# One encoder layer on one core: a sixth Strassen group in the input projection, tanh for the gates, bias and mask summed behind FFN 1, and weights cast and loaded earlier

## The chip, the core and the metric

The kernel runs on one core of one Trainium2 chip. Time is device time in microseconds (us) of one launch; a kernel's time is the median over its runs. The core has a matrix engine (PE), a vector engine (DVE), a scalar engine that evaluates functions (ACT), a general engine (POOL) and a queue processor that issues most transfers (SP). Each engine works through its own list of instructions in order; between engines they wait on semaphores.

## The reference

One layer of an encoder for 1024 tokens of width 1024, all in float32:

```python
h = x + 0.5 * swiglu(rms_norm(h, ffn1_norm), w_gate1, w_up1, w_down1)    # FFN 1, inner width 2816
u = rms_norm(h, mix_norm)
qa, ka, va, qb, kb, vb, ga, gb = split(u @ w_in)                          # 512 x 3, 512, 128, 128, 1024, 1024
ya = neighbourhood_attention_2d(qa, ka, va, na_rpb)     # 8 heads of 64; a learned bias per head and a window mask
yb = windowed_gqa_sink(rope(qb), rope(kb), vb, sink)    # 8 query heads, 2 key heads; a sink logit in the denominator
merged = sigmoid(ga) * (ya @ w_branch_a) + sigmoid(gb) * (yb @ w_branch_b)
h = h + merged @ w_out
h = h + 0.5 * swiglu(rms_norm(h, ffn2_norm), w_gate2, w_up2, w_down2)    # FFN 2
y = rms_norm(h, final_norm)
```

Tokens form a grid of 16 rows by 64 columns. In branch A a query sees a neighbourhood of 8 by 16 tokens, in branch B a band of 128 tokens to each side.

## The kernel before, in words

**Products in three parts.** A float32 operand is cast into a high part, and what is left is its low part (`split`, L93 the cast on ACT, L94 the subtraction on DVE, or on POOL where one is named). Each product is the sum of high by high, high by low and low by high: three matmuls, L145, L147 and L149 in `mm3`. PE writes into eight PSUM banks, four tagged `d` and four tagged `g`.

**Strassen.** Large matrix products run as seven block products (P1 to P7) in place of eight. `products` does this for a weight that is streamed in: the FFNs' gate and up weights, and the *groups* of the input projection. A group holds 4 of the 34 channel blocks of 128 channels that `w_in` has; its products are 7 x 2 x 4 x 3 = 168 matmuls of 128x512. Its weights land in `raw` or `ahead` tiles, ACT casts them (L309) and DVE subtracts (L312) into `ws` tiles, of which there are eight. `Down` does the FFNs' down products (and `w_out`): 7 products x 11 elements for the FFN; an element is one pair of left and right blocks with 12 matmuls of 128x512. `Down.prep` makes an element ready: load of the left block (L547), additions of the right blocks (L561, L563 on DVE; L564, L566 on POOL), two splits (L94). It runs RING = 7 elements ahead of PE. Functions in `loads` of an element are called in `run` just before that.

**Stages in time.** FFN 1 (to about 432 us), FFN 1 down (to 645), the transition with norm and transposes, the groups of the input projection (to 845), attention (to 1118), the rest of the branches, `w_out`, and FFN 2 from about 1180. `behind(prods)` runs group 0's first products between the transition's tokens, and loads the weights of groups 1 and 2 into `ahead` tiles (L286) at tokens 3 and 4; these tiles are of the `ws` kind.

**Attention.** 64 *units*: 32 of branch B (two heads, 128 queries each), then 32 of branch A. A unit is `scores` (two products per head, then a fused DVE step L1298 that adds bias or mask and takes the maximum, ACT's exp at L1301, DVE's reciprocal L1304 and scaling L1305), `turn` (transposes on PE, L1314, and splits of what they give, L94) and `values` (products, L1328 and L1333, then a copy of ACT, L1267, and additions of DVE, L1268 and L1271). Between the units `filling` feeds PE with *fill steps* from `filler`: first the channel blocks of ga and gb that are in no group ("gates", 8 steps of 6 matmuls 128x512 each), then `branch_b` (yb @ w_branch_b, 8 column blocks of 4 steps of 6 matmuls), then the start of branch A. There are 112 + 32 + 6 = 150 steps; 106 of them run between the units, 44 behind the last one. For each pair of heads of branch A, `load_bias` fetches the bias (made during FFN 1, in `bias_d`) and DVE adds the mask (L1088). `split_y` casts a block of ya or yb; it subtracts on POOL for six of the eight blocks.

**Order.** The order of instructions on each engine is that of the code, but for a scheduler that may move them within what the tiles allow; `pin` keeps an instruction in its place.

Of the kernel before, what the change touches and what calls it, by code (L numbers as in the profile page):

```python
# [36 lines left out]
def trunk_kernel(ctx, tc, x, xt, n1, wg1, wu1, wd1, nm, win, rpb, sink, wa, wb, wo,  # L37
# [54 lines left out]
    def split(dst_hi, dst_lo, src, eng=None):  # L92
        nc.scalar.copy(dst_hi, src)  # L93
        (eng or nc.vector).tensor_tensor(dst_lo, src, f32v(dst_hi), op=ALU.subtract)  # L94
# [139 lines left out]
    def products(src, n, after, at_end, extra, ring, by_hand=False, last=PRODUCTS):  # L234
# [34 lines left out]
        def load_ahead(i):  # L269

            for m in range(2):
                ahead[i, m] = main.tile([P, 1024], F32, tag="ws", bufs=8, name=nm_("ahead"))
                fetch(ahead[i, m], i, m, 0)
# [14 lines left out]
        def pieces(q):  # L288

            i, p, m = seq[q]  # L290
            if i and (i, p, m) in early:
                a = ahead[i, m][:, 512 if p == "P2" else 0:][:, :512]
# [95 lines left out]
    def behind(prods):  # L388

        run, load_ahead = prods[2:4]  # L390

        def post(t):
            if t >= 3:
                drain(run, 10)
            if t in (3, 4):
                load_ahead(t - 2)

        return post
# [278 lines left out]

    def behind_ffn1(n):
        down.at_end(n)
        if n <= 60 and spread:  # L680
            nc.sync.dma_start(*spread.pop(0))
# [194 lines left out]
    groups = [[(12, 13), (14, 15)], [(16, 17), (0, 1)], [(4, 5), (8, 9)], [(2, 3), (6, 7)], [(10, 11), (18, 19)]]  # L876
# [62 lines left out]

    pin = tc.keep_in_program_order  # L940
# [65 lines left out]

    def keep_u():

        h, l = rhs(T4)
        for i in range(2):  # L1010
            r = raw4()
            nc.sync.dma_start(r.rearrange("p (t f) -> p t f", t=2), u_d[2 * i:2 * i + 2].rearrange("t p f -> p t f"))
            cols = slice(i * 256, i * 256 + 256)
            v = [a[:, :, cols].rearrange("p c (t x) -> p c t x", t=2) for a in (h, l)]
            split(v[0], v[1], r.rearrange("p (t c x) -> p c t x", t=2, c=4))
# [41 lines left out]
    hook(2, gate_first)  # L1057
    hook(1, keep_u)
    pg = products(lambda i, m, half: w_cols(win[0], groups[i][m][half] * P), NG, store_z, at_end, (2, 3), range(8, 16),
                  last=("P1", "P2", "P5", "P6", "P7", "P4", "P3"))  # L1060
    down.into(transition(down1, gain, to_strassen, behind(pg), 2), pg)
# [4 lines left out]
    mask_a = masks[:, :768].rearrange("p (s k) -> p s k", s=2)  # L1066
    mask_b = masks[:, 768:]
    nc.sync.dma_start(mask_a, c_mask_a.rearrange("s p k -> p s k"))
# [12 lines left out]
    def bias_slot(s):  # L1081
        return fa[:, 768 * s:768 * s + 768].rearrange("p (e k) -> p e k", e=2)

    def load_bias(s, h):
        braw = raw4()[:, :384]
        nc.sync.dma_start(braw, bias_d[h])
        for e in range(2):
            nc.vector.tensor_tensor(bias_slot(s)[:, e, :].rearrange("p (d r w) -> p d r w", d=3, r=ROWS),  # L1088
                                    braw.rearrange("p (r d w) -> p d r w", d=3, w=8),
                                    mask_a[:, e, :].rearrange("p (d r w) -> p d r w", d=3, r=ROWS), op=ALU.add)  # L1090
# [58 lines left out]
    def branch_w(w, dc, eng=None, r=None):  # L1149

        t = ws4()
        if r is None:
            r = fetch_branch(raw4()[:, :512], w, dc)
        split(t[:, :512], t[:, 512:], r, eng)
# [15 lines left out]
    def split_y(slots, r0, eng):  # L1170
# [6 lines left out]
        split(h, l, r, eng)  # L1177

    a_order = [dc for p in range(4) for dc in (p, p + 4)]
    a_mm, a_raw = [], {}  # L1180

    def branch_a(i):

        w = branch_w(wa[0], a_order[i], nc.gpsimd, a_raw.get(i))
        bs = [bank("gd"[i % 2]) for _ in range(2)]
        a_mm.append((bs, branch_mm(bs, w, Y_A)))
# [4 lines left out]
    def gate_b(dc):  # L1191
        rb = xs4()
        nc.sync.dma_start(rb, g_d[D + dc * P:D + (dc + 1) * P, :])
        nc.scalar.activation(rb, rb, AF.Sigmoid)
        return rb

    def branch_b():

        for c in range(2, 4):
            split_y(Y_B[c], c * P, nc.vector if c == 2 else nc.gpsimd)  # L1200
        for g in (4, 6):
            new_ar(g, F32)
        nxt = branch_w(wb[0], 0, nc.vector), gate_b(0)
        for dc in range(NC8):
            w, rb = nxt
            bs = [bank("dg"[dc % 2]) for _ in range(2)]
            yield from branch_mm(bs, w, Y_B)
            if dc + 1 < NC8:
                nxt = branch_w(wb[0], dc + 1, nc.vector), gate_b(dc + 1)
            for n in range(2):  # L1210
                sl = slice(n * 512, (n + 1) * 512)
                nc.vector.tensor_tensor(merged(dc)[:, sl], bs[n], rb[:, sl], op=ALU.mult)

    def filler():
        for dc, nxt in zip(gates, gates[1:] + [None]):
            if nxt is not None:
                yield from gate(dc, {4: lambda: mix.update(gate=load_w(win[0], GA + nxt * P))})
            else:
                yield from gate(dc, {0: lambda: [fetch_y(c * P) for c in range(2)],
                                     4: lambda: [split_y(Y_B[c], c * P, nc.gpsimd) for c in range(2)],  # L1220
                                     5: lambda: [fetch_y(c * P) for c in range(2, 4)]})
        yield from branch_b()
        for i in range(2):
            branch_a(i)
            for _ in range(3):
                drain(a_mm[i][1], 1)
                yield

    fill = filler()
    nfill = len(gates) * 8 + 38  # L1230
# [7 lines left out]
    def units_b():  # L1238
        for j in range(NTT):
            for c in range(4):  # L1240
                def write(o, j=j, c=c):

                    if c == 0:
                        ybox["b"] = xs4()[:, :512].rearrange("p (c t) -> p c t", c=4)
                    lo = mix["lo"][:HD, c % 2]
                    nc.scalar.copy(lo, o[HD:])
                    for s in range(2):
                        nc.vector.tensor_tensor(ybox["b"][s * HD:s * HD + HD, c, :], o[:HD, s, :], lo[:, s, :], op=ALU.add)
                    if c == 3:
                        nc.gpsimd.dma_start(y_d[:512, j * P:(j + 1) * P].rearrange("(c p) t -> p c t", p=P), ybox["b"])  # L1250
# [4 lines left out]
                           sink=[nsk[:, 2 * c + s:2 * c + s + 1] for s in range(2)], write=write)  # L1255

    def units_a():
        for hp in range(4):
            qs, kd, kl, va = heads_a[hp]
            for s in range(2):  # L1260
                load_bias(s, 2 * hp + s)
            for j in range(NTT):
                def write(o, j=j, hp=hp):
# [8 lines left out]
                    if j in (3, 7) and hp < 3:  # L1272
                        cols = slice((j - 3) * P, (j + 1) * P)
# [298 lines left out]
```

## Time and profile before

| | us |
|---|---|
| median of 3 runs | 1932.24 |
| fastest to slowest | 1932.03 to 1932.97 |
| the profiled execution | 1934.2 |
| its span in the profile | 1932.4 |
| PE busy in it | 1921.6 |
| DVE, ACT, POOL busy | 1435.8, 943.4, 294.9 |

The profiled execution is one run with the hardware profiler on, 2.0 us above the median. Busy times of PE overlap, since matmuls are pipelined: what one costs is read from the distance of their starts. The same holds, in part, for DVE and ACT. An arrow in a row stands for what an engine waited for.

### The profile page before, as it was taken

The numbers are of one execution on the slowest core, as the hardware profiler recorded it, in microseconds if no ns is written. First come the engines' busy times: TensorE is split into PE (matmuls) and PEld (weight loads), VectorE is DVE, ScalarE is ACT, GpSimd is POOL, SyncE is SP. The second block draws the span as 40 slices with busy tenths as digits, with TensorE's granted clock in tenths as the row PEclk, the third lists the DMA queues.
The fourth block names the chain that finished last, engine by engine and source line by source line (L and its number), as shares of the span: only waits on it lengthen the run. The fifth ranks groups of instructions, "written<-read, shape, count | busy, mean of one in ns | idle before, by whom it ended". The sixth has DMA issues, their size and how long they took to land.

```text
span 1932.4 us, 25477 instructions
## 1 busy us (share of the span) xinstructions
PE 1921.6 (99%) x8956; PEld 1603.9 (83%) x8956; DVE 1435.8 (74%) x2560; ACT 943.4 (49%) x1826; POOL 294.9 (15%) x432
## 2 busy tenths in 40 slices
PE   9999999999999999999999999999999999999998
PEld 7888888888888888888888888888888888888886
DVE  7987765668957778678888856889676566569864
ACT  6532333344446543477778872365333333344453
POOL 0011110013400112211122222010111001005210
PEclk9999999999999999999999999999999999999999
DMA  6244323286333467653358675543422322493341
GB/s 262 100 167 162 130 106 126 87 292 224 89 109 135 161 202 239 218 163 104 106 135 197 190 241 207 175 153 120 147 93 104 131 86 106 144 356 99 113 143 61
DMA packets 151745, 298.70 MB, mean 155 GB/s; under 512 B 14912, under 2 KB 64448, under 8 KB 151616
## 3 DMA queue, kind: packets, MB, share of 16 engines
q1 hardware_dynamic: 123072, 210.53, 33.3%
q0 software_dynamic: 27824, 85.48, 13.2%
q8 instruction: 71, 1.16, 0.3%
q10 hardware_dynamic: 720, 1.05, 0.1%
q14 instruction: 58, 0.48, 0.1%
HBM read 210.50 MB, written 88.27 MB: 155 GB/s over the span
## 4 chain that ended last, share of the span: by engine, by line
PE 97%; DVE 1%; ACT 1%; DMA 1%; issue 0%; POOLq 0%; POOL 0%; DVEq 0%
PE g L145 18%; PE g L147 18%; PE g L149 18%; PE d L145 12%; PE d L149 12%; PE d L147 12%; PE d L1314 2%; PE g L1328 1%; PE d L1293 1%; PE d L1294 1%; PE g L1333 1%; PE d L138 1%; DMA ahead<-in_w_in_dram 0%; DVE ar L94 0%; DMA n1c<-in_ffn_norm_dram 0%
## 5 line engine op out<-in xcount | busy, mean ns | idle before, releaser
L145 PE MATMUL g<-ar,ws 128*128 128x512 f32 x1128 | 422.8, 395 | 0.6 <-DVE fa L602 0.6
L147 PE MATMUL g<-ar,ws 128*128 128x512 f32 x1128 | 417.1, 390 | 0.0
L149 PE MATMUL g<-ar,ws 128*128 128x512 f32 x1128 | 416.6, 390 | 0.0
L145 PE MATMUL d<-ar,ws 128*128 128x512 f32 x736 | 282.7, 391 | 0.4 <-ACT ws L309 0.4
L147 PE MATMUL d<-ar,ws 128*128 128x512 f32 x736 | 282.2, 390 | 0.4 <-DVE ar L813 0.3
L149 PE MATMUL d<-ar,ws 128*128 128x512 f32 x736 | 281.9, 390 | 0.0
L147 PEld LDWEIGHTS g<-ar,ws 128*128 128x128 f32 x1128 | 211.8, 188 | 44.9 <-DVE ar L834 0.4
L149 PEld LDWEIGHTS g<-ar,ws 128*128 128x128 f32 x1128 | 211.8, 188 | 45.0
L145 PEld LDWEIGHTS g<-ar,ws 128*128 128x128 f32 x1128 | 206.4, 188 | 36.7 <-ACT ar L93 1.0
L312 DVE TENSOR_TENSOR ws<-raw,ws 128x512 fp32r<-128x512 f32 x204 | 139.5, 690 | 99.1 <-ACT ws L309 98.1
L309 ACT CAST ws<-raw 128x512 fp32r<-128x512 f32 x204 | 125.0, 620 | 142.1 <-PE g L149 64.0
L147 PEld LDWEIGHTS d<-ar,ws 128*128 128x128 f32 x736 | 138.4, 188 | 30.0 <-DVE ar L813 1.3
L145 PEld LDWEIGHTS d<-ar,ws 128*128 128x128 f32 x736 | 138.4, 188 | 29.4 <-ACT ws L309 0.8
L149 PEld LDWEIGHTS d<-ar,ws 128*128 128x128 f32 x736 | 138.5, 188 | 29.2 <-DVE ws L312 0.5
L93 ACT CAST ws<-raw 128x512 fp32r<-128x512 f32 (+1 forms) x121 | 81.0, 669 | 144.1 <-PE d L149 63.7
L94 DVE TENSOR_TENSOR ws<-raw,ws 128x512 fp32r<-128x512 f32 (+1 forms) x119 | 93.2, 785 | 60.0 <-ACT ws L93 59.6
L415 POOL DMA_DIRECT2D hid<-fx x91 | 49.1, 540 | 432.0 <-DVE fx L475 287.9
L93 ACT CAST ar<-raw 128x512 fp32r<-128x512 f32 (+1 forms) x83 | 56.1, 679 | 94.3 <-PE g L147 55.0
L94 DVE TENSOR_TENSOR ws<-ar,ws 128x512 fp32r<-128x512 f32 x114 | 98.2, 867 | 2.8 <-ACT ws L93 2.8
L145 PE MATMUL g<-ws,ws 128*128 128x512 f32 x232 | 90.9, 392 | 0.0
L149 PE MATMUL g<-ws,ws 128*128 128x512 f32 x232 | 90.5, 390 | 0.0
L147 PE MATMUL g<-ws,ws 128*128 128x512 f32 x232 | 90.4, 390 | 0.0
(313 smaller groups left out, 3606.9 us busy)
## 6 DMA issues: line engine op xcount, KB each, us to landing
raw<-hid SPq DMA_DIRECT2D x70, 512.0 KB
hid<-fx POOLq DMA_DIRECT2D x91, 256.0 KB, 2.3
ar<-in_ffn_w_down_dram SPq DMA_DIRECT2D x32, 512.0 KB
raw<-in_ffn_w_up_dram SPq DMA_DIRECT2D x31, 512.0 KB
raw<-in_ffn_w_gate_dram SPq DMA_DIRECT2D x27, 512.0 KB
raw<-in_w_in_dram SPq DMA_DIRECT2D x27, 512.0 KB
hid<-fa POOLq DMA_DIRECT2D x51, 256.0 KB, 2.6
ar<-zs_d POOLq DMA_DIRECT2D x48, 256.0 KB, 5.0
```

The source lines that it names most:

```text
L93: nc.scalar.copy(dst_hi, src)
L94: (eng or nc.vector).tensor_tensor(dst_lo, src, f32v(dst_hi), op=ALU.subtract)
L138: nc.tensor.transpose(pt[:, c * P:(c + 1) * P], xs[:, (half * 4 + c) * P:(half * 4 + c + 1) * P], ident)
L145: nc.tensor.matmul(b, lhs[0], r[0], start=first, stop=False, **kw)
L147: nc.tensor.matmul(b, lhs[0], r[1], start=False, stop=False, **kw)
L149: nc.tensor.matmul(b, lhs[1], r[0], start=False, stop=last, **kw)
L309: nc.scalar.copy(w[0][:, :512], a)
L312: nc.vector.tensor_tensor(w[0][:, 512:], a, f32v(w[0][:, :512]), op=ALU.subtract)
L415: nc.gpsimd.dma_start(hid[PRODUCTS.index(p), i], src)
L1293: nc.tensor.matmul(b[:, :nw], un["q"][s], un["kd"][s][:, k0 * P:k1 * P], start=True, stop=False)
L1294: nc.tensor.matmul(b[:, :nw], un["q"][s], un["kl"][s][:, k0 * P:k1 * P], start=False, stop=True)
L1314: nc.tensor.transpose(pt[:, i * P:(i + 1) * P], un["pr"][s][:, i * P:(i + 1) * P], ident)
```

## The change

Six things change together.

1. Channel blocks 20 to 23 leave the gates and form a sixth group; gates are 80 steps in place of 112.
2. Gates open by tanh: sigmoid(x) = (1 + tanh(x/2)) / 2. ACT evaluates tanh(x/2); DVE's multiplication becomes (t + 1) * product in one instruction; the factor 0.5 goes into the scale of `w_out`'s evictions (`Down(4, wo[0], 0.5, ...)`).
3. Bias and mask of all eight heads are summed behind FFN 1's down products: at elements 8 + 5h a fetch (L700), at 11 + 5h two additions on DVE (L705), at 13 + 5h two writes to `bm_d` (L711). Attention then only loads the sums, into four places of `fa` and four held `hs` tiles, so `mask_a` is not loaded there.
4. Group 1's first weights, and half of group 2's, go into `hs` tiles, of which six are free then, and all loads ahead are issued at tokens 0 and 1 (L279, L295).
5. The branches' weights are loaded some steps and cast one block ahead (`fetch_w`, `split_w`), gates too (`fetch_gate`, `open_gate`); the subtractions of `split_y` all go to DVE; those of branch A's weights go to POOL from block 10 on only. u's put-back operand is loaded at hook 5 (`fetch_u`).
6. Fill steps are spread otherwise: 80 gate steps over the first 50 units, 28 steps of `branch_b` over the last 14; 10 steps are left behind the units. In branch B's units the two additions of 64x128 become one of 64x256, and the sink columns of both heads are copied at once.

```diff
+            for i, n in zip((1, 2), sooner or (3, 4)):
+                if t == n:
+                    load_ahead(i)
...
+    for h in range(8):
+        down.loads.setdefault(8 + 5 * h, []).append(lambda d, h=h: bias_fetch(h))
+        down.loads.setdefault(11 + 5 * h, []).append(lambda d, h=h: bias_add(h))
+        down.loads.setdefault(13 + 5 * h, []).insert(0, lambda d, h=h: bias_put(h))
...
-    groups = [[(12, 13), (14, 15)], [(16, 17), (0, 1)], [(4, 5), (8, 9)], [(2, 3), (6, 7)], [(10, 11), (18, 19)]]
+    groups = [[(12, 13), (14, 15)], [(16, 17), (0, 1)], [(4, 5), (8, 9)], [(2, 3), (6, 7)], [(10, 11), (18, 19)],
+              [(20, 21), (22, 23)]]
...
-    down.into(transition(down1, gain, to_strassen, behind(pg), 2), pg)
+                  last=("P1", "P2", "P5", "P6", "P7", "P4", "P3"), early_rooms=(1, (2, 0)))
+    down.into(transition(down1, gain, to_strassen, behind(pg, (0, 1)), 2), pg)
...
+    def open_gate(dc):
+        r = mix["rb", dc]
+        pin(nc.scalar.activation(r, r, AF.Tanh, scale=0.5))
+
+    def split_w(i):
+        mix["w", i] = branch_w(nc.gpsimd if i >= 10 else None, mix.pop(("wr", i)))
...
-            yield from branch_mm(bs, w, Y_B)
-            if dc + 1 < NC8:
-                nxt = branch_w(wb[0], dc + 1, nc.vector), gate_b(dc + 1)
+            mm = branch_mm(bs, mix.pop(("w", dc)), Y_B)
+            for c in range(4):
+                drain(mm, 1)
+                yield
+                if c == 0:
+                    if dc == 0:
+                        split_y(Y_B[3], 3 * P, nc.vector)
+                        open_gate(0)
+                    if dc + 1 < NC8:
+                        fetch_gate(dc + 1)
+                elif c == 1:
+                    split_w(dc + 1)
+                    fetch_w(dc + 2)
+                elif c == 3 and dc + 1 < NC8:
+                    open_gate(dc + 1)
...
-                nc.vector.tensor_tensor(merged(dc)[:, sl], bs[n], rb[:, sl], op=ALU.mult)
+                nc.vector.scalar_tensor_tensor(out=merged(dc)[:, sl], in0=rb[:, sl], scalar=1.0, in1=bs[n],
+                                               op0=ALU.add, op1=ALU.mult)
...
-    rate = (nfill - 44) / 64.0
-    spent = 3.0
+    n_b = 50
+    rates = (len(gates) * 8 / n_b, 28 / (64.0 - n_b))
+    spent = 0.0
...
-            split_y(Y_A[n - 60], 512 + (n - 60) * P, nc.gpsimd)
+            split_y(Y_A[n - 60], 512 + (n - 60) * P, nc.vector)
```

Three places show what stands where on an engine. The first is DVE in FFN 1's down products, where it makes elements of the third product ready. `raw` is a left block, `ar` and `xs` hold right blocks; the scheduler has put the additions of a later product's right blocks (L563) between the splits. Before:

```order
L561 TENSOR_TENSOR ar_3099<-ar_3478,ar_3099 128x512
L94 TENSOR_TENSOR ws_3643<-raw_3548,ws_3643 128x512
L94 TENSOR_TENSOR ws_3644<-ar_3094,ws_3644 128x512
L563 TENSOR_TENSOR ar_3094<-ar_3099,ar_3094 128x512
L94 TENSOR_TENSOR ws_3662<-raw_3548,ws_3662 128x512
L94 TENSOR_TENSOR ws_3663<-ar_3094,ws_3663 128x512
```

The same engine at the same product after the change, where `hs` holds bias, mask and their sum:

```order
L98 TENSOR_TENSOR ws_3860<-raw_3700,ws_3860 128x512
L98 TENSOR_TENSOR ws_3861<-ar_3100,ws_3861 128x512
L705 TENSOR_TENSOR hs_3483<-hs_3482,hs_3479 128x384
L705 TENSOR_TENSOR hs_3484<-hs_3482,hs_3480 128x384
L574 TENSOR_TENSOR ar_3100<-xs_3815,ar_3100 128x512
L98 TENSOR_TENSOR ar_561<-raw_3740,ar_561 128x512
```

Two additions of 128x384 stand between the splits of one element and the next, at every fifth element; the other rows are as before.

The second place is SP around the loads ahead. Before, they stand among the writes of h (L937) and of u (L220) of the transition:

```order
L937 DMA h_d<-fa 128x1024 x3
L286 DMA ahead_4965<-in_w_in_dram 128x8x128
L220 DMA u_d<-s_494_4927 128x512
L286 DMA ahead_4967<-in_w_in_dram 128x8x128
L286 DMA ahead_5057<-in_w_in_dram 128x8x128
L286 DMA ahead_5059<-in_w_in_dram 128x8x128
```

After, on the same queue, most of them stand among the left blocks of FFN 1's down products (L558):

```order
L711 DMA bm_d<-hs_3483 128x384
L711 DMA bm_d<-hs_3484 128x384
L279 DMA ahead_4587<-in_w_in_dram 128x4x128
L279 DMA ahead_4590<-in_w_in_dram 128x4x128
L279 DMA ahead_4591<-in_w_in_dram 128x4x128
L279 DMA ahead_4634<-in_w_in_dram 128x4x128
L558 DMA raw_4343<-hid 128x2x512
L279 DMA ahead_4635<-in_w_in_dram 128x4x128
```

They moved ahead of the transition, behind the last writes of the bias sums.

The third place is DVE in the last units. Before, it holds only what the units themselves need (ISA is the fused step with the maximum):

```order
L1298 ISA fa,nmx_10066<-d_10074,fa 128x256
L1298 ISA nmx_10066 128x1
L1268 TENSOR_TENSOR s_691_6540<-g_10055,s_691_6540 64x256
L1271 TENSOR_TENSOR fa<-g_10055,s_691_6540 64x128 x2
L1304 RECIPROCAL rc_10068<-ssum_10067 128x2
L1305 TENSOR_SCALAR fa<-fa,rc_10068 128x256
L94 TENSOR_TENSOR ws_10088<-d_10090,ws_10088 128x3x128
L94 TENSOR_TENSOR ws_10089<-d_10096,ws_10089 128x3x128
```

After, on DVE at the same unit:

```order
L98 TENSOR_TENSOR ws_10308<-d_10315,ws_10308 128x3x128
L1372 ISA fa,nmx_10342<-d_10350,hs_6850 128x256
L1372 ISA nmx_10342 128x1
L1269 SCALAR_TENSOR_TENSOR ar_9562<-raw_10198,d_10299 128x512
L98 TENSOR_TENSOR ar_561<-raw_10257,ar_561 128x1024
L1339 TENSOR_TENSOR s_722_6846<-g_10331,s_722_6846 64x256
L1378 RECIPROCAL rc_10344<-ssum_10343 128x2
L1339 TENSOR_TENSOR s_722_6846<-g_10388,s_722_6846 64x256
L1342 TENSOR_TENSOR fa<-g_10331,s_722_6846 64x128 x2
L1379 TENSOR_SCALAR fa<-fa,rc_10344 128x256
```

A gate's multiplication (L1269) and a split of ya (128x1024) now stand between the unit's steps.

More of the change, by code (lines that the diff above doesn't have):

```diff
@@ L1079, in trunk_kernel, with bias_at, fetch_bias @@
     heads_a = {}
[L1081 to L1090, printed above, removed]
+    held = [main.tile([P, 512], F32, tag="hs", bufs=6, name=nm_("hs")) for _ in range(6)]
+    def bias_at(hp, s, e):
+        k = 2 * (hp % 2) + s
+        return held[k][:, :384] if e else fa[:, 384 * k:384 * k + 384]
+    def fetch_bias(hp):
+        for s in range(2):
+            for e in range(2):
+                nc.sync.dma_start(bias_at(hp, s, e), bm_d[2 * hp + s, e])
     def prep_a(hp):
@@ L1224, in filler @@
             branch_a(i)
-            for _ in range(3):
+            for c in range(3):
                 drain(a_mm[i][1], 1)
                 yield
+                if c == 0:
+                    split_w(NC8 + 1 + i)
+                    fetch_w(NC8 + 2 + i)
+                    a_fetch(i)
+        split_w(NC8 + 3)
+        for i in range(2):
+            a_open(i)
     fill = filler()
-    nfill = len(gates) * 8 + 38
     def small(name, n=2):
@@ L1362, in trunk_kernel @@
             drain(prep, 1)
-        filling(0.5)
+        filling(n)
         if len(pipe) > 1 and pipe[1] is not None:
```

163 lines of the change are left out of this document (96 added, 67 removed).

## The prediction

> **What bounds the kernel now.** I read the page first, then windows of each stage, the waits of PE, and the timeline where PE waits or nearly waits. The page:
>
> ```profile
> span 1932.4 us, 25477 instructions
> PE 1921.6 (99%) x8956; PEld 1603.9 (83%) x8956; DVE 1435.8 (74%) x2560; ACT 943.4 (49%) x1826; POOL 294.9 (15%) x432
> PE 97%; DVE 1%; ACT 1%; DMA 1%; issue 0%; POOLq 0%; POOL 0%; DVEq 0%
> L145 PE MATMUL g<-ar,ws 128*128 128x512 f32 x1128 | 422.8, 395 | 0.6 <-DVE fa L602 0.6
> ```
>
> PE is busy nearly throughout, and the chain that ended last is PE for 97%. So the end moves by the matmuls removed and by the gaps of PE that come or go. A matmul's listed 395 ns overlaps the next one; its price comes from a window of FFN 2, where PE never waits:
>
> ```profile
> 1400.00:1600.00 200.00, 200.00 (x884) 165.69 (x883) 128.07 (x196) 73.59 (x126) 19.93 (x37) 1.00 0.28 100
> ```
>
> Columns are the window, then busy time and count of PE, weight loads, DVE, ACT and POOL, the granted clock (1.00), and DMA. 200 / 884 = 0.2262 us per matmul of 128x512.
>
> The waits of PE that count, and their causes in the timeline:
>
> ```profile
> PE g L145 <- DVE fa L602: 0.6, 1, 0.6
> PE d L145 <- ACT ws L309: 0.4, 1, 0.4
> PE d L1314 <- DVE ws L94: 0.3, 1, 0.3
> ...
> 654.43 0.62 ACT L309 CAST ws<-ahead 128x512 fp32r<-128x512 f32 x1 [2.86 <-DMA ahead<-in_w_in_dram]
> 655.08 0.69 DVE L312 TENSOR_TENSOR ws<-ahead,ws 128x512 fp32r<-128x512 f32 x1 [2.08 <-ACT ws L309]
> 655.69 0.68 DVE L602 SCALAR_TENSOR_TENSOR fa<-g,fa 128x512 f32<-128x512 f32 x1
> 656.52 0.47 PE L145 MATMUL g<-ar,ws 128*128 128x512 f32 x1 [0.64 <-DVE fa L602]
> 678.08 0.50 PE L145 MATMUL d<-ar,ws 128*128 128x512 f32 x1 [0.41 <-ACT ws L309]
> ```
>
> In the transition a load ahead lands late: ACT waits 2.86 us for it, DVE 2.08 us for ACT, an eviction (L602) queued behind that on DVE is late, and PE stands 0.64 us; with DVE behind, PE stands 0.41 us more at 678.08.
>
> **The change, part by part.**
>
> *Sixth group.* Four gates go: 4 x 8 steps x 6 matmuls = 192. A group comes: 168. 24 fewer, x 0.2262 = **-5.43 us**, all on PE's path. Weights (four channel blocks either way), casts and evictions are off that path; PE waited for none of them in the earlier groups behind 678 us.
>
> *Loads sooner.* Group 1's weights, and half of group 2's, are issued among FFN 1's left blocks, by the elements they stand at some 90 us ahead of their use. Both waits above have the late load as cause: -0.64 - 0.41 = **-1.05 us**. Ends: 0 (the wait at 656.52 is for DVE, which could be late for another reason) and -1.4, counting from start to start of the matmuls, with the slower restart.
>
> *Bias and mask behind FFN 1.* This looks free, since PE is the bound there, but it isn't. In the stretch where POOL adds right blocks DVE has no idle time:
>
> ```profile
> 454.00:521.00 67.00, 67.00 (x298) 55.46 (x297) 65.76 (x68) 28.59 (x50) 35.55 (x22) 1.00 0.30 100
> ...
> 479.15 0.69 DVE L561 TENSOR_TENSOR ar<-ar,ar 128x512 f32<-128x512 f32 x1
> 479.76 0.68 DVE L94 TENSOR_TENSOR ws<-raw,ws 128x512 fp32r<-128x512 f32 x1
> 480.36 1.78 DVE L94 TENSOR_TENSOR ws<-ar,ws 128x512 fp32r<-128x512 f32 x1
> 482.18 0.69 DVE L561 TENSOR_TENSOR ar<-ar,ar 128x512 f32<-128x512 f32 x1
> ...
> 479.92 1.67 POOL L564 TENSOR_TENSOR ar<-xs,ar 128x512 f32<-128x512 f32 x1 [1.36 <-DVE ar L561]
> ...
> 518.85 1.78 DVE L94 TENSOR_TENSOR ar<-ar,ar 128x512 fp32r<-128x512 f32 x1
> ...
> 522.12 0.39 PE L147 MATMUL g<-ar 128*128 128x512 f32 x1
> ```
>
> DVE is busy 65.76 of 67 us. A subtraction that costs 0.60 us (start to start) takes 1.78 us while one of POOL's 22 additions runs; an element takes DVE 3.03 us (479.15 to 482.18) against PE's 12 x 0.2262 = 2.71. So DVE loses the lead that the 7 elements it may run ahead give it: the split that ends at 518.85 + 1.78 = 520.63 is read by the matmul at 522.12, by its tile, and the lead is down to 1.49 us. In DVE's new order four pairs of additions stand between 454 us and that split. Their price, from the same addition in attention:
>
> ```profile
> 939.89 1.02 DVE L1088 TENSOR_TENSOR fa<-raw,masks 128x384 f32<-128x384 f32 x2
> 940.85 0.17 DVE L1304 RECIPROCAL rc<-ssum 128x2 f32<-128x2 f32 x1
> ```
>
> 0.96 / 2 = 0.48 us each. DVE is saturated, so 8 x 0.48 = 3.84 us is its delay, of which the lead covers 1.49: PE waits **+2.35 us** near 522. Low end 1.1 (the pairs fill the 67 - 65.76 = 1.24 us of idle time); high end if each addition also collides with one of POOL (8 x 1.18 more): +11.8. I take the low price, because POOL's number of additions doesn't change and the pairs stand ahead of the addition (L572, L574) that releases POOL. Behind the pair SP's writes wait for DVE, and left blocks queue behind these; the loads themselves wait for later DVE splits anyway: nothing. From 521 on, without POOL, two splits of 0.60 per element let DVE regain 1.5 us of each 2.71, and a pair takes 0.96 at every fifth: nothing.
>
> [...]
>
> *Attention.* Units 50 to 62, then 60 to 62, then the heaviest earlier block:
>
> ```profile
> 1061.80:1117.92 56.12, 56.12 (x336) 49.41 (x335) 48.31 (x154) 48.81 (x121) 12.16 (x10) 1.00 0.57 174
> 1106.70:1117.92 11.22, 11.22 (x71) 10.01 (x70) 9.13 (x32) 10.72 (x27) 2.13 (x3) 1.00 0.36 124
> 996.49:1020.09 23.60, 23.60 (x146) 21.05 (x145) 21.94 (x66) 18.65 (x49) 6.85 (x14) 1.00 0.53 145
> ...
> 1125.52 0.58 DVE L1271 TENSOR_TENSOR fa<-g,s 64x128 f32<-64x128 f32 x2
> 1126.13 1.44 DVE L94 TENSOR_TENSOR ws<-raw,ws 128x512 fp32r<-128x512 f32 x1
> 1127.49 1.21 DVE L94 TENSOR_TENSOR ar<-raw,ar 128x1024 fp32r<-128x1024 f32 x1
> 1128.63 0.41 DVE L1268 TENSOR_TENSOR s<-g,s 64x256 f32<-64x256 f32 x1
> L94 POOL TENSOR_TENSOR ar<-raw,ar 128x1024 fp32r<-128x1024 f32 x4 | 9.9, 2478 | 19.5 <-ACT ar L93 19.5
> ```
>
> In units 50 to 62 DVE gets, by the new order, 13 gate multiplications and 7 splits of 512 columns (0.60 each, as above) and 5 splits of 1024 (1.14, from 1127.49 to 1128.63); it loses 2 splits of 1024 and 4 additions of 0.48. 12.0 + 5.7 - 2.3 - 1.9 = +13.5, so 61.8. PE has 2 fill steps per unit in place of 106 / 64 = 1.66: 13 x 0.34 x 6 x 0.2262 = +6.0, so 62.1. DVE is then as loaded as PE. In units 60 to 62: DVE 9.13 + 3 x 1.14 + 5 x 0.60 = 15.6, PE 11.22 + 1.4 = 12.6; the 3.0 us between can't be hidden, since no slack precedes it and the last unit's transposes need these results. For the waits inside the 13 units I add 1.5, little, because at 93% DVE (21.94 of 23.60) PE's waits in all of attention are the 0.3 us listed above. **+4.5 us**. Ends: +1 (work moves behind the last unit, where 10 fill steps stand) and +7.4, if DVE keeps its idle time there (56.12 - 48.31 = 7.8) beside the new work.
>
> POOL's subtractions (2.48 us, on no chain) go; the 13 us or so that branch B's units save on DVE buy nothing, PE being the longer there. ACT gets 7 gates' tanh inside the units and loads one function table less; it was busy 48.81 of 56.12, with gate copies leaving. The 36 more SP transfers hide under a DMA share of 0.3 to 0.57. A tanh costs what a sigmoid cost, the 0.5 in an eviction's scale nothing.
>
> *Sum.* -5.43 - 1.05 + 2.35 + 4.5 = +0.4 us. The profiled execution stood at 1934.2, 2.0 above the median; against the median of 1932.24 the sum gives **1932.6**. A difference within 0.2% (3.9 us) is what a measurement of this kernel hardly tells from none: 1928.4 to 1936.1.
>
> **The rivals.**
>
> *Both queues absorb it (faster).* The pairs cost 1.1 near 522 and attention 0.3, as its waits now: -6.48 + 1.4 = -5.1, 1927.2. For: PE's waits in attention are tiny at 93% DVE. Against: 3.84 is more than the 1.49 of lead, by two plain rows.
>
> *DVE sets the pace in units 50 to 63 (slower).* If its idle time of 7.8 us there (it waits for exp sums, scores and casts of the same unit) stays, those units last 69.6 in place of 62.1: -6.48 + 2.35 + 7.5 = +3.4, 1935.6, or 1937.1 with the forecast's 1.5 of waits on top. It passes the bound from 8.0 us on. Against: DVE's waits shorten when it is behind.
>
> *Each bias addition is blocked by POOL (slower).* -6.48 + 11.8 + 4.5 = +9.8, 1942. From four blocked additions on (4.7) the kernel is over the bound. For: 1.78 against 0.60 in every element. Against: 22 POOL additions before and after.
>
> *The early loads don't do what they say.* If DVE's queue, not the load, makes L602 late at 656.52, the 1.05 us stay: 1933.7.
>
> **How the numbers follow.** The forecast has 0.45, the early-loads rival 0.07, absorption 0.18, DVE's pace 0.20 (half of it above 1936.1), blocked additions 0.10. Faster: 0.18, and 0.02 from the forecast's low ends. Slower: 0.10 + 0.10, and 0.06 from the forecast's high ends. Same: the rest, 0.54. The range is 1927 to 1939: it takes in absorption and DVE's pace, and leaves out blocked additions and some of either end.
>
> **What would show it.** PE's waits: none at 656 and 678; one or several on DVE near 522, 2 to 3 us together; 3 us or so at the last units, on L1269, L98 or the scaling steps of DVE. Counts: 24 matmuls fewer. Bias additions listed near 0.55 us; if near 1.7, the blocking rival holds. If the window of units 50 to 63 exceeds 63 us by over 6, DVE sets the pace. The prediction fails if another stage has PE waits: the sixth group's weights, or gates fetched too late for tanh.

## The result: 0.6% slower, and the profile after

| | before | after |
|---|---|---|
| median of 6 runs, us | 1933.24 | 1944.00 |
| lowest to highest | 1932.03 to 1934.08 | 1941.95 to 1946.07 |
| the profiled execution, and its span | 1934.2, 1932.4 | 1943.68, 1941.9 |

The ratio is 1.0059 (95% interval 1.0048 to 1.0069). The forecast of 1932.6 was wrong, and the time lies above the range's 1939. From the page of the changed kernel, its span, the busy times by engine, and the shares of the chain that ended last:

```profile
span 1941.9 us, 25522 instructions
PE 1920.5 (99%) x8932; PEld 1599.6 (82%) x8932; DVE 1450.2 (75%) x2529; ACT 944.4 (49%) x1836; POOL 283.2 (15%) x428
PE 87%; DVE 5%; issue 5%; DMA 1%; POOL 0%; ACT 0%; POOLq 0%; SPq 0%; DVEq 0%
```

PE has 24 matmuls fewer, but the chain that ended last is PE for 87% only, in place of 97%. PE's waits in the changed kernel, those of 0.4 us and more (us in total, times, the longest):

```profile
PE d L1388 <- issue: 3.2, 1, 3.2
PE d L1388 <- DVE fa L1379: 2.0, 1, 2.0
PE d L1159 <- DMA raw<-z_d: 1.8, 1, 1.8
PE d L151 <- DVE ar L98: 1.7, 3, 0.8
PE d L149 <- DVE ws L98: 1.6, 2, 1.2
PE g L773 <- POOL ident masks.py:199: 1.4, 1, 1.4
PE d L149 <- ACT ws L95: 0.8, 2, 0.4
...
PE d L149 <- ACT ar L95: 0.4, 1, 0.4
```

The wait of 1.4 us at the start of the kernel was there before. Waits are listed from the end of the modelled matmul; below I use *gaps*: what the distance from one matmul's start to the next has above the usual one for its size (0.2262 us for 512 columns), where it is above 0.15 us, summed by stage from the trace. All in us; "3 in hand" and the other names are those of the experiments that follow.

| kernel | to 500 | FFN 1 down, 500 to 600 | transition and groups, to 846 | start of attention, to 900 | to 1080 | end of attention, to 1180 | rest |
|---|---|---|---|---|---|---|---|
| before | 2.8 | 0.2 | 1.6 | 0.0 | 1.0 | 0.0 | 0.4 |
| after | 2.8 | 1.3 | 0.5 | 4.6 | 0.2 | 9.3 | 0.4 |
| 3 in hand | 2.7 | 1.3 | 0.4 | 1.6 | 0.6 | 2.8 | 1.8 |
| start only | 2.6 | 1.1 | 0.4 | 1.2 | 0.0 | 7.7 | 0.6 |
| one step sooner | 1.8 | 1.3 | 0.5 | 1.8 | 0.6 | 9.7 | 0.4 |
| splits on POOL | 3.3 | 1.1 | 0.5 | 4.1 | 0.2 | 10.5 | 1.2 |
| even fill | 2.8 | 0.9 | 0.6 | 1.0 | 0.6 | 10.0 | 0.8 |
| 3 in hand, bias later | 1.8 | 0.0 | 0.5 | 1.1 | 0.6 | 2.8 | 1.8 |
| the same and early columns | 2.7 | 0.0 | 0.5 | 0.5 | 0.6 | 2.8 | 1.7 |

From before to after, attention (846 to 1180) goes from 1.0 to 14.1. The account of the two spans: -5.4 for the matmuls, +1.1, -1.1, +13.1, together +7.7. The spans differ by 9.5, so 1.8 are left; breaks below 0.15 us go with it (149 of 0.06 to 0.11 us, 13.6 us in all, in place of 128 and 11.7; between 1080 and 1180 us there are 39 in place of 13).

### The profile page after: what moved, and what is told of

The parts are those of the page before. It is cut to its first block, busy times and chain, and to the rows that moved or that the text cites. A ratio compares the mean times of both kernels' runs of the same rounds, so it can differ in the third digit from the quotient of the medians.

```text
span 1941.9 us, 25522 instructions
## 1 busy us (share of the span) xinstructions
PE 1920.5 (99%) x8932; PEld 1599.6 (82%) x8932; DVE 1450.2 (75%) x2529; ACT 944.4 (49%) x1836; POOL 283.2 (15%) x428
## 3 DMA queue, kind: packets, MB, share of 16 engines
q0 software_dynamic: 27888, 85.48, 13.6%
q10 hardware_dynamic: 720, 1.05, 0.1%
## 4 chain that ended last, share of the span: by engine, by line
PE 87%; DVE 5%; issue 5%; DMA 1%; POOL 0%; ACT 0%; POOLq 0%; SPq 0%; DVEq 0%
PE g L149 16%; PE g L151 16%; PE g L153 16%; PE d L149 11%; PE d L153 11%; PE d L151 11%; PE d L1388 2%; DVE ws L98 2%; DVE ar L98 1%; PE g L1407 1%; PE d L1369 1%; PE d L1370 1%; PE g L1402 1%; PE d L142 1%; DMA raw<-z_d 1%
## 5 line engine op out<-in xcount | busy, mean ns | idle before, releaser
L149 PE MATMUL g<-ar,ws 128*128 128x512 f32 x1096 | 415.2, 394 | 0.0
L151 PE MATMUL g<-ar,ws 128*128 128x512 f32 x1096 | 409.9, 390 | 0.1
L153 PE MATMUL g<-ar,ws 128*128 128x512 f32 x1096 | 409.6, 390 | 0.0
L149 PE MATMUL d<-ar,ws 128*128 128x512 f32 x760 | 294.1, 392 | 3.0 <-DVE ws L98 1.6
L151 PE MATMUL d<-ar,ws 128*128 128x512 f32 x760 | 292.8, 391 | 1.4 <-DVE ar L98 0.8
L153 PE MATMUL d<-ar,ws 128*128 128x512 f32 x760 | 291.9, 391 | 0.1
L151 PEld LDWEIGHTS g<-ar,ws 128*128 128x128 f32 x1096 | 205.8, 188 | 43.5 <-DVE ar L874 0.6
L153 PEld LDWEIGHTS g<-ar,ws 128*128 128x128 f32 x1096 | 205.8, 188 | 43.3
L149 PEld LDWEIGHTS g<-ar,ws 128*128 128x128 f32 x1096 | 201.5, 188 | 36.0 <-DVE fa L971 0.3
L322 DVE TENSOR_TENSOR ws<-raw,ws 128x512 fp32r<-128x512 f32 x210 | 143.6, 689 | 107.7 <-ACT ws L319 106.8
L149 PEld LDWEIGHTS d<-ar,ws 128*128 128x128 f32 x760 | 142.4, 188 | 33.9 <-issue 1.5
L151 PEld LDWEIGHTS d<-ar,ws 128*128 128x128 f32 x760 | 142.8, 188 | 31.5 <-DVE ar L98 1.5
L153 PEld LDWEIGHTS d<-ar,ws 128*128 128x128 f32 x760 | 142.7, 188 | 30.3 <-DVE ws L322 0.5
L95 ACT CAST ws<-raw 128x512 fp32r<-128x512 f32 (+1 forms) x107 | 70.5, 659 | 134.0 <-PE d L153 58.4
L98 DVE TENSOR_TENSOR ws<-raw,ws 128x512 fp32r<-128x512 f32 (+1 forms) x107 | 83.9, 784 | 46.7 <-ACT ws L95 46.5
```

The costliest lines, as they stand in the source:

```text
L95: hi = nc.scalar.copy(dst_hi, src)
L149: nc.tensor.matmul(b, lhs[0], r[0], start=first, stop=False, **kw)
L151: nc.tensor.matmul(b, lhs[0], r[1], start=False, stop=False, **kw)
L153: nc.tensor.matmul(b, lhs[1], r[0], start=False, stop=last, **kw)
L322: nc.vector.tensor_tensor(w[0][:, 512:], a, f32v(w[0][:, :512]), op=ALU.subtract)
```

## The experiments

Every run has a run of the kernel before on the same chip; each ratio is to that.

**The start of attention.** The timeline of the changed kernel there (start, duration, engine; in brackets what the engine waited before, and for what):

```profile
882.38 0.54 POOL L945 DMA_DIRECT2D g_d<-fa  x1 [4.68 <-DVE fa L971]
887.42 0.39 PE L151 MATMUL g<-ar,ws 128*128 128x512 f32 x1
888.65 0.48 DVE L1372 CUSTOM_DVE_ANT_0 fa<-d,masks,nsk 128x256 f32<-128x256 f32 x1 [3.29 <-DMA g_d<-fa]
891.01 0.66 PE L1388 MATMUL d<-ident,fa 128*128 128x128 f32 x2 [3.21 <-issue]
```

The last group's write from `fa` to `g_d`, issued at 882.38, is still reading the columns to which a fused step of DVE is to write its scores. It lands 6.1 us after its issue; DVE waits 3.29 us, and PE has no work until the first transposes at 891.01. Before, the same kind of wait was there, 0.82 us on a write to `z_d` that was issued at 842.32 and landed 5.7 us later:

```profile
848.18 0.48 DVE L1298 CUSTOM_DVE_ANT_0 fa<-d,masks,nsk 128x256 f32<-128x256 f32 x1 [0.82 <-DMA z_d<-fa]
```

But DVE had a split of 1.23 us to do between the two fused steps there, and `filling` began with 3.0 fill steps in hand (`spent = 3.0`), which the change set to 0.0. First run:

```diff
-    spent = 0.0
+    spent = 3.0
```

> The changed kernel, but filling starts with 3.0 fill steps in hand, as before the change, in place of 0.0; 7 steps are left behind the units in place of 10. Theory A (a transfer out of fa and too few fill steps beside it): the first fused steps of attention write places of fa that the last group's writes to g_d still read (wait of DVE on DMA g_d<-fa, 3.3 us); three steps, 3 x 6 x 0.2262 = 4.1 us, then cover this, and the gap of PE at 891 (3.4 us) shrinks to under 0.8: 1944.0 becomes about 1940.5. With the block loads of yb two units sooner the V load may also find its buffer sooner: 2.0 us less again at most. Theory B (DVE is short of time all through attention): steps moved to the front are missing at the end, the sum of gaps stays: 1943 to 1945.

Measured 1935.33, ratio 1.0011 (1.0002 to 1.0021). This one line gives back 8.7 of the 10.8 us, where theory A expected 3.5, or 5.5 at most. DVE's wait is still there in that run, and longer:

```profile
DVE fa L1372 <- DMA g_d<-fa: 3.7, 1, 3.7
```

So the steps in hand do not shorten it; they give PE work beside it. The table shows where the gain stands: 3.0 at the start, and 6.5 at the end of attention, which I had not put down to it. The next run parts the two:

```diff
-    rates = (len(gates) * 8 / n_b, 28 / (64.0 - n_b))
-    spent = 0.0
+    rates = (77 / n_b, 28 / (64.0 - n_b))
+    spent = 3.0
```

> The changed kernel with 3.0 fill steps in hand at the start, and 77 / 50 per unit after that in place of 80 / 50, so that branch B's steps stand at the same units as in the changed kernel and 10 steps are left. It parts the two things that 3.0 in hand did. Theory A1 (the gain of 8.7 us came from the start alone): 1935 to 1936. Theory A2 (the start gives the gap at 891 only, 3.4 less the 1.1 that stays; the rest came because branch B's steps and the loads of yb, V and the gates stand three steps sooner): the gaps from 1094 to 1171 us and the wait for V's load stay as in the changed kernel, 9 us together: about 1941.

Measured 1938.93, ratio 1.0030 (1.0020 to 1.0039): between the two theories. The start is repaired (4.6 to 1.2), the V load's wait is down to 0.3, and the gaps in front of branch B's blocks stay as expected. By the medians 5.1 of the 8.7 us come with the cover at the start, and 3.6 because branch B's steps stand three steps sooner.

Is it the write out of `fa`? I took the wait away by other columns for the first two units:

```diff
-        both = fa[:, 1536 + 2 * (npair[0] % 2) * (384 + ext):][:, :2 * (384 + ext)].rearrange("p (s k) -> p s k", s=2)
+        base = (3072, 0)[npair[0]] if npair[0] < 2 else 1536 + 2 * (npair[0] % 2) * (384 + ext)
+        both = fa[:, base:][:, :2 * (384 + ext)].rearrange("p (s k) -> p s k", s=2)
```

> The changed kernel, in which only the first two units of attention write their scores to other columns of fa: unit 0 to columns from 3072 on, unit 1 from 0 on, both written out by the last group some 7 us earlier or more. Nothing else moves. Theory (the fused step waits because the last writes to g_d still read columns 2048 to 3072): the wait of DVE on DMA g_d<-fa (3.3 us) goes, the gap of PE at 891 (3.4 us) falls below 0.8, and the V load's wait of about 2 us stays: 1940.7. Rival (the first scores are late for another reason, such as casts of the keys): the gap stays, 1944.

Measured 1943.43, ratio 1.0049 (1.0036 to 1.0063): a miss, and the timeline of that run shows the reason:

```profile
883.30 0.17 DVE L1367 COPY fa<-nsk 128x2 f32<-128x2 f32 x1 [5.81 <-DMA g_d<-fa]
...
885.85 0.39 PE L1371 MATMUL d<-ar,ar 128*128 128x256 f32 x1 [4.02 <-DVE ar L98]
```

The new place was still being written out too, and what touches it first is the copy of the sink columns, which stands on DVE ahead of splits that PE needs. The same change in a kernel that has 3 in hand and the bias later (a run of that kernel follows below):

> The kernel with 3.0 fill steps in hand and the later bias work (1932.9), with the first two units' scores in other columns of fa as well. The gap of 0.6 us that is left at 886 goes: 1932.3; unchanged if three steps already cover the wait and the 0.6 us are the handoff from score to transpose.

Measured 1937.18, ratio 1.0019 (1.0010 to 1.0028), 3.2 us of gap at 881: the copy again. In the changed kernel, with columns that were written out some 12 us before the first score:

```diff
-        both = fa[:, 1536 + 2 * (npair[0] % 2) * (384 + ext):][:, :2 * (384 + ext)].rearrange("p (s k) -> p s k", s=2)
+        base = 770 * npair[0] if npair[0] < 2 else 1536 + 2 * (npair[0] % 2) * (384 + ext)
+        both = fa[:, base:][:, :2 * (384 + ext)].rearrange("p (s k) -> p s k", s=2)
```

> The changed kernel, in which the first two units of attention write their scores to fa columns 0 to 769 and 770 to 1539. The last group wrote those out from 855 to 872 us on, some 12 us before the first score; the place tried before, from column 3072 on, was written out at 876 and 877 us, which was too late for the copy of the sink columns that DVE does first. Theory (the fused step, and that copy, wait for writes out of fa): no wait of DVE on DMA g_d<-fa above 1 us, the gap of PE at 891 (3.4 us) and the half clock behind it (some 1.5 us) go, the V load's wait and the gaps of the last 14 units stay: 1939 to 1940.5. Rival (the start of attention lacks fill steps whatever the place): 1943 to 1944.

Measured 1941.06, ratio 1.0041 (1.0026 to 1.0055). Part of it: the gap at the start falls from 3.4 to 2.2. Now the third unit's copy (it still goes to the old columns) waits, by the waits of DVE in that run:

```profile
DVE fa L1367 <- DMA g_d<-fa: 3.2, 1, 3.2
```

It stands on DVE ahead of the first units' reciprocals. So writes out of `fa` hold DVE up at whatever touches the columns first, for 3.2 to 5.8 us in these runs, and three fill steps (18 matmuls, 4.1 us) cover most of it: 1.6 us of gaps are left at the start beside the wait of 3.7. That is shown; what a kernel with no such wait would take at the start was not reached.

**The end of attention.** First the load of DVE, which my forecast had as the cause:

```diff
-            split_y(Y_A[n - 60], 512 + (n - 60) * P, nc.vector)
+            split_y(Y_A[n - 60], 512 + (n - 60) * P, nc.gpsimd)
```

and the same for three of the four blocks of yb.

> The changed kernel, with the subtractions of split_y on POOL as before the change (all but the third block of yb). Theory A (DVE is the bound in the last 14 units): seven times 1.14 us leave DVE, of these 4 to 5 among units 50 to 62; the gaps of PE on DVE from 1094 to 1171 us (7.3 us together) fall by 3 to 5: about 1940. Rival (these gaps come from late loads and casts of ACT, and POOL takes 2.48 us in place of 1.14): the splits end later, PE waits longer for them at the start of branch B, 1944 to 1947.

Measured 1944.38, ratio 1.0058 (1.0041 to 1.0075), as the rival has it. (The edit moves six splits, not the seven that the expectation counts.) The gaps don't fall in sum (10.5 in place of 9.3), but they move. Among the waits of PE there are

```profile
PE d L1159 <- DMA raw<-z_d: 3.2, 1, 3.2
PE d L1369 <- DVE ws L98: 2.6, 1, 2.6
PE d L1388 <- DVE ar L1269: 0.8, 1, 0.8
```

and 1.6 in three waits on `ws`: the last unit's transposes wait 0.8 in place of 2.0, V's load costs 3.2 in place of 1.8, and 2.6 stand at a unit's scores where nothing stood. DVE's capacity is not what is short: in the changed kernel it is busy 66.5 of the 76.2 us from 1094.9 to 1171.1, by its windows (from and to, length, then busy us and instructions of PE, PEld, DVE, ACT and POOL, the granted clock, the DMA share and GB/s). In the run with 3 in hand it is busier, 72.6 of 79.0 us (second row), and the gaps from 1080 to 1180 are 2.8 in place of 9.3:

```profile
1094.90:1171.10 76.20, 69.05 (x387) 57.60 (x387) 66.54 (x185) 60.10 (x140) 2.21 (x4) 1.00 0.56 180
1088.00:1167.00 79.00, 77.36 (x437) 65.67 (x436) 72.59 (x206) 66.39 (x156) 5.37 (x10) 1.00 0.72 204
```

Four of the gaps (0.56, 0.56, 0.56 and 1.39 us) stand in front of the same matmul, the first of a branch B block whose sums go to `d` banks, right behind a unit's scores (L1369, L1370), which go to `d` banks too, as the timeline of the changed kernel has the last of them:

```profile
1158.38 0.34 PE L1370 MATMUL d<-ar,ar 128*128 128x384 f32 x1
1158.64 0.69 DVE L98 TENSOR_TENSOR ws<-hs,ws 128x512 fp32r<-128x512 f32 x1
1159.24 1.02 DVE L98 TENSOR_TENSOR ws<-d,ws 128x384 fp32r<-128x384 f32 x2
1159.94 0.47 PE L149 MATMUL d<-ar,ws 128*128 128x512 f32 x1 [1.23 <-DVE ws L98]
```

PE waits until DVE has read the transposes out of their `d` bank (ws<-d), and on DVE that stands behind a weight split (ws<-hs). The third gap is the same; at the second ACT's cast out of a `d` bank ends last, and at the first a weight's cast (ws<-hs on ACT), 0.02 us behind DVE's reading of the scores. To test it, branch B's blocks one fill step sooner than in the run with 77 / 50:

```diff
-    rates = (77 / n_b, 28 / (64.0 - n_b))
+    rates = (78 / n_b, 28 / (64.0 - n_b))
```

> The kernel with 3.0 fill steps in hand and 77 / 50 per unit after that (1938.9), with 78 / 50: branch B's steps stand one fill step sooner, half a unit. In the changed kernel and in the one with 77 / 50 each block of branch B whose sums go to banks of kind d begins right behind a unit's two score products, which take d banks too; one step sooner it begins behind the transposes or the values. Theory (the gaps ahead of these blocks, 0.56 + 0.56 + 0.55 + 1.39 = 3.1 us at 1089 to 1153, are waits for a d bank that DVE and ACT still read): they go but for one at most, 1936. Rival (what counted in the kernel at 1935.3 was that everything stood three steps sooner): one step gives a third of it or nothing, 1938 to 1939, and the gaps stay ahead of the same matmuls.

Measured 1940.43, ratio 1.0035 (1.0021 to 1.0050). In the trace three of the four gaps go (one of 0.3 is left of the last), and so does the 2.2 us at the last unit's transposes. So these gaps go with the place of the block behind the scores, as the theory of the banks has it. But the time got no better, 1940.43 against 1938.93 with intervals that overlap: one new gap of 5.0 us stands there. The waits of PE in that run, and those of ACT:

```profile
PE d L149 <- ACT ar L95: 5.4, 2, 4.8
```

```profile
ACT ar L95 <- DMA raw<-y_d: 5.1, 1, 5.1
```

The split of a yb block waits for its load, which is issued at 1089.03 and lets ACT begin at 1102.0 only; the DMA engines are busy for 90% or more in all but one of the slices of 0.5 us between. In the changed kernel it is V's load that is late there: it is issued at 1097.73, 10.4 us ahead of its use at 1108.15, while before it was issued at 1033.65, 31.5 us ahead of its use at 1065.2. By then loads of yb, from 1035 on, have taken `raw` buffers, of which there are four. That buffers and full DMA engines make one or the other late is my reading; no run changes either alone. And the spreading of fill steps as before:

```diff
-    rates = (len(gates) * 8 / n_b, 28 / (64.0 - n_b))
-    spent = 0.0
+    rates = (105 / 64.0, 105 / 64.0)
+    spent = 3.0
```

> The changed kernel, with its fill steps spread as before the change: 3.0 in hand and 105 / 64 = 1.64 per unit throughout, in place of 1.6 and then 2 per unit. Branch B's steps then begin some three units sooner. Theory A: the gap at 891 goes (as with 3.0 in hand alone), and DVE's extra work lies in 17 units in place of 14; the gaps from 1094 to 1171 fall by 1 to 3: about 1938.5 to 1940. Theory B (DVE short all through): no gain beside the start, or a loss in the last units, where PE has 1.64 steps in place of 2 to wait beside: 1941 to 1944.

Measured 1941.31, ratio 1.0046 (1.0031 to 1.0061): the start is repaired, the end is not (10.0, a gap of 3.3 at the last unit's transposes among it). Spreading thinner is no cure here.

**FFN 1 down.** The additions behind POOL's stretch:

```diff
-        down.loads.setdefault(8 + 5 * h, []).append(lambda d, h=h: bias_fetch(h))
-        down.loads.setdefault(11 + 5 * h, []).append(lambda d, h=h: bias_add(h))
-        down.loads.setdefault(13 + 5 * h, []).insert(0, lambda d, h=h: bias_put(h))
+        down.loads.setdefault(25 + 3 * h, []).append(lambda d, h=h: bias_fetch(h))
+        down.loads.setdefault(28 + 3 * h, []).append(lambda d, h=h: bias_add(h))
+        down.loads.setdefault(28 + 3 * h, []).append(lambda d, h=h: bias_put(h))
```

> The changed kernel, with the bias work at elements 25 + 3h (fetch) and 28 + 3h (additions and writes) in place of 8 + 5h, 11 + 5h and 13 + 5h, so behind the stretch in which POOL adds right blocks. Theory A (the additions eat DVE's lead there): the gaps of PE from 517 to 524 us, 1.33 us together, go, and no new ones come, since DVE has 1.5 us to spare per element: 1942.7. Rival (they come from something else, such as later left blocks): the gaps stay.

Measured 1941.47, ratio 1.0048 (1.0033 to 1.0063). That is 2.5 us less by the medians, but the interval overlaps that of the changed kernel (1.0048 to 1.0069). What the trace shows is the 1.3 us: the gaps at 517 to 524 are gone, with none in their place.

**The sixth group and the early loads,** each undone in the kernel with 3 in hand:

```diff
-    groups = [[(12, 13), (14, 15)], [(16, 17), (0, 1)], [(4, 5), (8, 9)], [(2, 3), (6, 7)], [(10, 11), (18, 19)],
-              [(20, 21), (22, 23)]]
+    groups = [[(12, 13), (14, 15)], [(16, 17), (0, 1)], [(4, 5), (8, 9)], [(2, 3), (6, 7)], [(10, 11), (18, 19)]]
```

> The kernel with 3.0 fill steps in hand (1935.3), with the sixth group undone: channel blocks 20 to 23 are gates again, 112 gate steps over the first 50 units; all else stays. Theory A (24 matmuls are worth their 5.43 us): 1940.8 with the same gaps. Rival (more fill steps per unit, 2.24 in place of 1.6, cover gaps of attention, so the sixth group is worth less): 1936 to 1939, with fewer gaps from 850 to 1180 us.

Measured 1938.11, ratio 1.0023 (1.0014 to 1.0033): 2.8 us slower than with six groups by the medians (2.3 by the ratios), not 5.4, but the two intervals overlap. The rival is right in part: with 2.24 fill steps per unit the gaps at the start of attention are 0.6 (at 844.55, ahead of its first scores) in place of 1.6. Over the whole trace the gaps are 10.3 in place of 11.3, which leaves 4.4 of the 5.4; the rest is not explained.

```diff
-                  last=("P1", "P2", "P5", "P6", "P7", "P4", "P3"), early_rooms=(1, (2, 0)))
-    down.into(transition(down1, gain, to_strassen, behind(pg, (0, 1)), 2), pg)
+                  last=("P1", "P2", "P5", "P6", "P7", "P4", "P3"), early_rooms=())
+    down.into(transition(down1, gain, to_strassen, behind(pg), 2), pg)
```

> The kernel with 3.0 fill steps in hand, with the loads ahead back at tokens 3 and 4 and in ws tiles as before the change. Theory (their being early removed the gaps at 656 and 678 us): the two gaps come back, 0.80 + 0.57 less the 0.22 that the kernel has at 678 now: +1.15, 1936.5. Rival (DVE's queue makes them): 1935.3.

The waits of PE in that run have this line again:

```profile
PE g L149 <- DVE fa L613: 0.9, 1, 0.9
```

The gap at 657 is back (1.04 from start to start), that at 679 is 0.59 in place of 0.22, so 1.4 in the trace. The median is 1935.08, ratio 1.0009 (1.0000 to 1.0018), against 1935.33: a gain of 1.4 can't be told there from none.

**Towards a better version.** Both repairs together, the 3 in hand and the additions behind POOL's stretch:

> The kernel with 3.0 fill steps in hand, and the bias work at elements 25 + 3h and 28 + 3h. If gaps add up: 1935.3 less 1.2 (the gaps at 516 to 520 us) = 1934.1, between 0 and 2 us above the kernel before the change. If the order of attention is so tight that a shift of a microsecond moves other gaps, it can be anywhere from 1933 to 1937.

Measured 1932.90, ratio 0.9997 (0.9988 to 1.0006): level with the kernel before. In that kernel, 25 steps of branch B over the last 14 units:

```diff
-    rates = (len(gates) * 8 / n_b, 28 / (64.0 - n_b))
+    rates = (len(gates) * 8 / n_b, 25 / (64.0 - n_b))
```

> The kernel with 3.0 fill steps in hand and the later bias work (1932.9), with 25 steps over the last 14 units in place of 28, so that 10 are left behind the units again. Theory: the gap at 1212 (1.4 us, PE on the last gate multiplications) came with only 7 steps left and goes; DVE has 2 multiplications less to do among the units; but the units have 3 steps fewer to wait beside: 1931.5, or 1933 if gaps of the units grow by as much.

Measured 1935.80, ratio 1.0010 (1.0002 to 1.0019): the gap at 1212 goes and 4 us come at the end of attention, while the shift by three steps in the first run had taken 6.5 away. And both repairs with the early columns for the first two units:

> The kernel with 3.0 fill steps in hand and the later bias work (1932.9), with the same early columns of fa for the first two units. If the 0.6 and 0.5 us gaps left at 886 and 892 come from the writes out of fa: 1931.8 to 1932.3, faster than both kernels; if they are the handoffs from score to transpose: 1932.9.

Measured 1932.17, against 1933.96 for the kernel before on that chip: ratio 0.9993 (0.9984 to 1.0002). The 0.6 at 886 is gone, the 0.5 at 891 is not. It is the fastest kernel tried; by the interval it is not told from the one before.

## Why the prediction was wrong, step by step

*Sixth group, -5.43.* 24 matmuls fewer, as counted. Undoing it costs 2.8 by the medians and 4.4 by matmuls and gaps of the traces: the steps that leave attention had covered 1 us at its start. The forecast had no price for that; its exact size is not settled.

*Loads sooner, -1.05.* As forecast in the trace: no gap at 656, 0.31 left at 679, so 1.37 less 0.31 = 1.06 from start to start.

*Bias and mask, +2.35.* The mechanism was right, the size 1.3, in three gaps from 517 to 524 us that are gone in the run with the additions later. The window of POOL's stretch in the changed kernel:

```profile
454.00:521.00 67.00, 66.28 (x290) 53.87 (x288) 65.81 (x72) 27.86 (x50) 37.90 (x21) 1.00 0.39 129
```

and in its timeline two pairs of additions on DVE and the matmul behind them:

```profile
480.92 3.21 DVE L705 TENSOR_TENSOR hs<-hs,hs 128x384 f32<-128x384 f32 x2
499.06 1.01 DVE L705 TENSOR_TENSOR hs<-hs,hs 128x384 f32<-128x384 f32 x2
521.12 0.50 PE L151 MATMUL d<-ar 128*128 128x512 f32 x1 [0.83 <-DVE ar L98]
```

Three of four pairs took 1.0 us together, one 3.21, beside two additions of POOL. The rival in which POOL blocks each of them falls: there are 21 POOL additions in the window (22 before), and 21 instructions of DVE that take over 1 us (22 before), whichever stand there. The forecast chose the low price because POOL's number of additions does not change, and the trace bears that choice out.

*Attention, +4.5.* This is the step that failed. It measured +13.1 by gaps:

| term | forecast | measured |
|---|---|---|
| start of attention | 0 | 4.6 |
| last unit's transposes | 3.0 | 2.4 |
| waits of PE on DVE and ACT ahead of these | 1.5 | 4.9 |
| V's load | 0 | 2.0 |
| units from 900 to 1080 | 0 | -0.8 |

So the last unit was right in mechanism and nearly in size; what failed is the start, which had no term, V's load, which had none either, and the 1.5 for waits inside the units. I read DVE's load against PE's in a sum over 13 units, 61.8 against 62.1 us. The sum itself was good: DVE is busy 62.1 us from unit 50's reciprocal to unit 63's (1097.98 to 1169.64). But it does not decide here; this stretch lasts 71.7 us, and 64.3 with 3 in hand (1101.76 to 1166.01), where DVE is busy 59.4 us. What decides is which instruction stands in front of which: a first matmul behind the scores of a unit, a bank release behind a weight split, a copy behind a write. The three fill steps in hand were in the diff (`spent`), and the wait that they covered was in the profile of before, as 0.8 us of DVE on z_d<-fa; I gave the loss of this cover no price. My count of steps passed over them too: with 3.0 in hand 109 steps, not 106, run between the units before the change, and 41, not 44, are left.

A second cost was not in the working. The windows of the changed kernel beside the first gap (the granted clock is the third number from the end of a row):

```profile
880.00:887.00 7.00, 6.89 (x35) 5.62 (x34) 5.09 (x7) 4.12 (x6) 1.08 (x2) 1.00 1.12 332
887.00:891.00 4.00, 0.81 (x4) 0.36 (x3) 1.90 (x9) 1.12 (x5) 0.00 (x0) 0.95 0.56 178
891.00:892.00 1.00, 0.99 (x4) 0.82 (x5) 0.17 (x1) 1.00 (x5) 0.00 (x0) 0.50 0.00 0
893.00:894.00 1.00, 1.00 (x4) 0.83 (x4) 1.00 (x4) 0.34 (x1) 0.00 (x0) 0.50 0.00 0
894.00:895.00 1.00, 1.00 (x9) 0.90 (x8) 0.22 (x3) 0.43 (x2) 0.00 (x0) 0.99 0.00 0
```

After standing 3.4 us PE runs at half its clock for 3 us. Half of 3 us is 1.5 us of work lost, though PE was busy. Of this 1.0 us is in the gaps of the table, as matmuls 0.2 us or more apart too far.

*The rivals.* "Both queues absorb it" falls with the gaps. "Each bias addition is blocked" forecast 1942 and came nearest in time, by luck: its 9.4 us do not show. "DVE sets the pace" had its sign, since that stretch of 71.7 us is over 6 above 63, but not the cause: with 3 in hand it lasts 64.3 us with nearly as much work of DVE, and taking splits of 1.14 us off DVE gained nothing. "Early loads don't do what they say" falls. None had the start.

Open: why branch B's steps three sooner take gaps of 4.9 us away at the end (7.7 to 2.8), while one step sooner puts a late load in their place; and how much of the wide spread of the changed kernel's runs (1941.95 to 1946.07, against 1932.03 to 1934.08) comes from the clock and how much from loads that land at different times. The mean granted clock goes with it, 0.998 in the fastest run and 0.996 in the three slowest; by an estimate from these rounded means, 0.002 x 1942 = 3.9 us of clock, it could be most of the 4.1 us, but no run shows which gaps bring it.

## What to carry to other kernels

Where two engines hand work to each other every few microseconds, a sum of busy time says little about gaps: go through the order at the few places where the change removes fill, and ask of each wait in the old profile, however small, what covered it. A count of work in hand at a loop's start is such a cover; it looks like a rounding constant and was worth 8.7 us here. And an engine that is idle a quarter of the time over the kernel can be full in one stage (DVE, busy 75% of the changed kernel's span, was busy 65.81 of the 67 us from 454 to 521): move work only behind the stretch in which its lead over the bound engine shrinks.

## What the hardware did that I had not expected

- PE lost its clock over gaps inside the kernel: granted 0.50 for 3 us behind a gap of 3.4. The length of a gap alone does not settle it: behind a gap of 2.2 us the clock was halved in one run and not in another. The same gap of 2.2 us at the last unit's transposes left the clock at 1.00 in the changed kernel, and at 0.50 in the run with the first other columns. The window of the changed kernel, and that of the other run:

```profile
1171.00:1172.00 1.00, 0.96 (x4) 0.70 (x5) 0.85 (x3) 0.98 (x3) 0.00 (x0) 1.00 0.88 251
```

```profile
1171.00:1172.00 1.00, 1.00 (x3) 0.81 (x3) 1.00 (x3) 0.51 (x2) 0.00 (x0) 0.50 1.02 298
```

- A 256 KB write from SBUF lands in 2.3 us in FFN 1 of the kernel before (hid<-fx on its page, the median of 91); the one from `fa` that DVE waits for took 6.1 us (issued at 882.38), beside loads, in a stretch where the DMA share is 1.12 (880 to 887). The last group's four writes ahead of 875 us landed in 2.3 to 3.0 us, the four behind in 5.3 to 7.8. That the loads are the cause was not tested.
